# Cross-entropy over 32,000 classes: column sums of the last exps moved from ScalarE to VectorE, and the loads re-cut

## Chip, cores, metric

One core of a Trainium2 chip. The metric is the device time of one execution in microseconds (us), as a median over executions. All executions used here were with a granted clock of 1.0.

## The reference

```python
batch, num_classes = 256, 32000        # logits fp32, labels int32
log_probs = logits - np.max(logits, axis=-1, keepdims=True)
log_probs = log_probs - np.log(np.sum(np.exp(log_probs), axis=-1, keepdims=True))
return np.array([-log_probs[i, labels[i]] for i in range(batch)])
```

The logits are 32.77 MB, read once. Kernels here leave the maximum out: they compute log(sum of exp(x) times exp(-x[label])).

## The kernel before

Each of 128 partitions holds two rows in a line, 64,000 columns. They are loaded in 14 pieces ("chunks" 0 to 13), exponentiated in place by ScalarE, whose accumulator also gives the chunk's sum over its columns. The sums of the second row lie as columns in `parts[1]`; VectorE adds these up, and TensorE multiplies the sum by a diagonal matrix of exp(-x[label]), which also turns 128 partitions into one row. The last chunk's sum is added by a second, accumulating matmul. ScalarE takes the log, and 1 KB is stored.

```python
CHUNKS = [
    14848, 12288, 8832, 6528, 4992, 3776, 2752,
    2368, 1856, 1344, 1344, 1152, 1024, 896,
]
# ... tiles: chunks 0 to 4 have their own, 5 (x_mid) reuses chunk 1's, 6 to 13 (x_tail) chunk 0's

    def exps(i):
        t, base = tiles[i]
        for a, b, r in pieces[i]:
            if i == len(CHUNKS) - 1:
                acc = s_last[:, :]
            else:
                acc = parts[r][:, seen[r]:seen[r] + 1]
                seen[r] += 1
            nc.scalar.activation(
                out=t[:, a - base:b - base],
                in_=t[:, a - base:b - base],
                func=AF.Exp,
                accum_out=acc,
            )
# ... loads, labels, diag
        for i in range(2, len(CHUNKS) - 1):
            exps(i)
            # ... first row's sum, matmul and log after chunk 4
        nc.vector.reduce_sum(out=sums[:, 1:2], in_=parts[1][:, :], axis=mybir.AxisListType.X)
        nc.tensor.matmul(lane[1][:, :], sums[:, 1:2], diag[1][:, :], start=True, stop=False)
        exps(len(CHUNKS) - 1)
        nc.tensor.matmul(lane[1][:, :], s_last[:, :], diag[1][:, :], start=False, stop=True)
        log_row(1)
        # ... store
```

The softmax here doesn't subtract the row's maximum and nothing guards it: scores larger than these inputs give would overflow.

## Time and profile before

| | before |
|---|---|
| time, median | 86.03 us (85.92 to 86.08, 4 runs) |
| span of the profiled run | 84.3 us |
| ScalarE / VectorE busy | 58.9 / 0.8 us |
| last load landed (the trace's landing records) | 80.29 us |
| log of the second row starts | 82.03 us |

The span runs from the first instruction to the last on the core; the time measured outside it is some 1.7 us longer. The lines behind the table are in the prediction below. What counts is the start of the second log: what follows it (0.27 us of log, then the store and the end of the program, 2.3 us together) is the same in all kernels here. In a profile line, ACT is ScalarE, DVE VectorE, PE TensorE (PEld its loading of weights) and SP the queue that issues the loads; L95 is a line of the kernel, `out<-in` names tiles, and what stands in brackets is the idle time before the instruction and what ended it. The landing records of the trace give the moment at which each of the sixteen DMA engines reported its share of a load; a load has landed with the last of them. The "taper" below is the row of ever smaller loads at the end.

### The profile page before, as it was taken

The page shows a single profiled execution, that of the slowest core. Times are in us where ns is not written, and L with a number is a line of the kernel's source. Part 1 is how long each engine was busy: PE and PEld are TensorE (multiplying, and loading weights), DVE is VectorE, ACT ScalarE, POOL GpSimd, SP SyncE. Part 2 cuts the span into 40 slices and gives each one's busy share as a digit, 9 for nine tenths or more (in the row PEclk, how much of TensorE's full clock was granted, in tenths as well). Part 3 has the DMA queues.
Part 4 walks back from the last instruction along what each step waited for, and adds up shares of the span by engine and source line. Part 5 has one row for each costly group of instructions (what it writes and reads, how often), then busy time and mean ns, then how long its engine had stood idle before and what let it go on. Part 6 is the DMA issues. An engine that isn't in the chain of part 4 may idle for free.

```text
span 84.3 us, 126 instructions
## 1 busy us (share of the span) xinstructions
PE 1.8 (2%) x6; PEld 0.3 (0%) x6; DVE 0.8 (1%) x4; ACT 58.9 (70%) x34; POOL 3.0 (4%) x10
## 2 busy tenths in 40 slices
PE   0000000000000000000000002000000000000050
PEld 0000000000000000000000000000000000000000
DVE  0000000000000000000000200000000000000000
ACT  6000000000899999189999999999999999999960
POOL 3000000000640000000000000000000000000000
DMA  9199999998889999699998999999999999999500
GB/s 394 56 451 451 451 451 451 451 451 373 373 373 466 536 443 396 291 503 402 436 486 372 433 396 409 451 436 401 401 449 408 416 427 416 410 414 406 211 0 0
DMA packets 2226, 32.77 MB, mean 389 GB/s; under 512 B 433, under 2 KB 434, under 8 KB 1202
## 3 DMA queue, kind: packets, MB, share of 16 engines
q1 hardware_dynamic: 2018, 32.77, 91.9%
q10 hardware_dynamic: 144, 0.00, 0.1%
q0 software_dynamic: 64, 0.00, 0.1%
HBM read 32.77 MB, written 0.00 MB: 389 GB/s over the span
## 4 chain that ended last, share of the span: by engine, by line
DMA 64%; issue 13%; another core or an unknown queue 12%; SPq 4%; ACT 3%; PE 1%
DMA x<-in_logits_dram 41%; DMA x_tail<-in_logits_dram 22%; SPq L83 4%; ACT x_tail L95 3%; PE lane L143 1%; ACT res L103 0%; ACT x L95 0%; ACT eg L131 0%
## 5 line engine op out<-in xcount | busy, mean ns | idle before, releaser
L95 ACT ACTIVATE x<-x 128x14848 f32<-128x14848 f32 (+5 forms) x6 | 40.7, 6790 | 21.6 <-DMA x<-in_logits_dram 21.6
L95 ACT ACTIVATE x_tail<-x_tail 128x1344 f32<-128x1344 f32 (+6 forms) x8 | 12.2, 1525 | 0.4 <-DMA x_tail<-in_logits_dram 0.4
L95 ACT ACTIVATE x_mid<-x_mid 128x3776 f32<-128x3776 f32 x1 | 3.4, 3350 | 0.0
L118 POOL DMA_INDIRECT g<-in_logits_dram,idx x2 | 2.1, 1037 | 0.6 <-issue 0.3
L74 ACT ACT_TABLE_LOAD x1 | 1.3, 1283 | 0.7 <-PEq L162 0.7
L138 PE MATMUL lane<-diag,sums 128*1 128x128 f32 x2 | 0.6, 397 | 51.2 <-DVE sums L137 51.2
L95 ACT ACTIVATION_READ_ACCUMULATOR x_tail<-x_tail 128x1 f32 x8 | 1.5, 186 | 0.0
L141 PE MATMUL lane<-diag,sums 128*1 128x128 f32 x2 | 0.6, 394 | 28.8 <-DVE sums L140 28.8
L95 ACT ACTIVATION_READ_ACCUMULATOR x<-x 128x1 f32 x6 | 1.1, 186 | 0.0
L103 ACT ACTIVATE res<-lane 1x128 f32<-1x128 f32 x2 | 0.5, 264 | 0.7 <-PE lane L143 0.7
L133 DVE TENSOR_SCALAR diag<-ident,eg 128x128 f32<-128x128 f32 x2 | 0.5, 284 | 46.8 <-ACT eg L131 46.8
L116 POOL TENSOR_TENSOR idx<-idx,lbl 128x2 int32<-128x2 int32 x1 | 0.2, 193 | 20.1 <-DMA lbl<-in_labels_dram 20.1
L143 PE MATMUL lane<-diag,s_last 128*1 128x128 f32 x2 | 0.6, 395 | 0.2 <-ACT x_tail L95 0.2
L140 DVE TENSOR_REDUCE sums<-parts 128x1 f32<-128x11 f32 x1 | 0.2, 165 | 29.3 <-ACT x_tail L95 29.3
masks.py:199 POOL TENSOR_SCALAR_AFFINE_SELECT ident<-ident 128x128 f32<-128x128 f32 x1 | 0.3, 292 | 0.1
L138 PEld LDWEIGHTS lane<-diag,sums 128*1 128x1 f32 x2 | 0.1, 80 | 51.2 <-DVE sums L137 51.2
masks.py:197 POOL MEMSET ident<- 128x128 f32 x1 | 0.2, 194 | 0.0
L137 DVE TENSOR_REDUCE sums<-parts 128x1 f32<-128x3 f32 x1 | 0.2, 156 | 3.7 <-ACT x L95 3.7
L131 ACT ACTIVATE eg<-g 128x2 f32<-128x2 f32 x1 | 0.2, 187 | 0.0
L95 ACT ACTIVATION_READ_ACCUMULATOR x_mid<-x_mid 128x1 f32 x1 | 0.2, 186 | 0.0
L141 PEld LDWEIGHTS lane<-diag,sums 128*1 128x1 f32 x2 | 0.1, 80 | 29.3 <-DVE sums L140 29.3
L114 POOL IOTA idx<- 128x2 int32 x1 | 0.1, 121 | 0.4 <-POOLq L162 0.4
(5 smaller groups left out, 0.5 us busy)
## 6 DMA issues: line engine op xcount, KB each, us to landing
x<-in_logits_dram SPq DMA_DIRECT2D x1, 7424.0 KB, 20.6
x<-in_logits_dram SPq DMA_DIRECT2D x1, 6144.0 KB, 34.9
x<-in_logits_dram SPq DMA_DIRECT2D x1, 4416.0 KB, 44.9
x<-in_logits_dram SPq DMA_DIRECT2D x1, 3264.0 KB, 52.2
x<-in_logits_dram SPq DMA_DIRECT2D x1, 2496.0 KB, 56.9
x_mid<-in_logits_dram SPq DMA_DIRECT2D x1, 1888.0 KB, 18.1
x_tail<-in_logits_dram SPq DMA_DIRECT2D x1, 1376.0 KB
x_tail<-in_logits_dram SPq DMA_DIRECT2D x2, 672.0 KB, 27.0
```

Source lines behind the costliest of these rows:

```text
L74: nc.scalar.preload_act_table_set("natural_log_exp_and_others")
L83: nc.sync.dma_start(out=t[:, a - base:b - base], in_=flat[:, a:b])
L95: nc.scalar.activation(out=t[:, a - base:b - base], in_=t[:, a - base:b - base], func=AF.Exp, accum_out=acc,)
L103: nc.scalar.activation(out=res[0:1, r:ROWS * P:ROWS], in_=lane[r][:, :], func=AF.Ln)
L116: nc.gpsimd.tensor_add(out=idx[:, :], in0=idx[:, :], in1=lbl[:, 0:2 * ROWS:2])
L118: nc.gpsimd.indirect_dma_start(out=g[:, r:r + 1], out_offset=None, in_=logits[:, :], in_offset=bass.IndirectOffsetOnAxis(ap=idx[:, r:r + 1 ...
L131: nc.scalar.activation(out=eg[:, :], in_=g[:, :], func=AF.Exp, scale=-1.0)
L133: nc.vector.tensor_scalar_mul(diag[r][:, :], ident[:, :], eg[:, r:r + 1])
L137: nc.vector.reduce_sum(out=sums[:, 0:1], in_=parts[0][:, :], axis=mybir.AxisListType.X)
L138: nc.tensor.matmul(lane[0][:, :], sums[:, 0:1], diag[0][:, :], start=True, stop=True)
L141: nc.tensor.matmul(lane[1][:, :], sums[:, 1:2], diag[1][:, :], start=True, stop=False)
L143: nc.tensor.matmul(lane[1][:, :], s_last[:, :], diag[1][:, :], start=False, stop=True)
```

## The change

The intent: an exp with accumulator costs ScalarE an extra instruction that reads the accumulator. Six of the last exps lose it, VectorE (idle) sums their columns instead, and ScalarE, now quicker on small pieces, gets smaller last loads, so that less is left to do after the last landing. As VectorE's sum of chunk 11 and ScalarE's of 12 and 13 come late, each gets its own matmul; with that of the sum of the parts there are four.

```diff
 CHUNKS = [
-    14848, 12288, 8832, 6528, 4992, 3776, 2752,
-    2368, 1856, 1344, 1344, 1152, 1024, 896,
+    14592, 13696, 9728, 7424, 4864, 3904, 2880,
+    2112, 1408, 1152, 832, 576, 448, 384,
 ]
+ON_VECTOR = range(6, 12)
+SINGLE = 11
...
-            if i == len(CHUNKS) - 1:
-                acc = s_last[:, :]
+            if i >= SINGLE:
+                acc = single[i][:, :]
...
-            nc.scalar.activation( ... func=AF.Exp, accum_out=acc)
+            x = t[:, a - base:b - base]
+            if i in ON_VECTOR:
+                nc.scalar.activation(out=x, in_=x, func=AF.Exp)
+                nc.vector.reduce_sum(out=acc, in_=x, axis=mybir.AxisListType.X)
+            else:
+                nc.scalar.activation(out=x, in_=x, func=AF.Exp, accum_out=acc)
...
-        for i in range(2, len(CHUNKS) - 1):
+        for i in range(2, SINGLE):
...
-        exps(len(CHUNKS) - 1)
-        nc.tensor.matmul(lane[1][:, :], s_last[:, :], diag[1][:, :], start=False, stop=True)
+        for i in (11, 12, 13):
+            exps(i)
+        for i in (12, 11, 13):
+            nc.tensor.matmul(lane[1][:, :], single[i][:, :], diag[1][:, :], start=False, stop=i == 13)
```

More of the change, by code (lines that the diff above doesn't have):

```diff
@@ L58 @@
         tiles.append((tail, starts[HEAD + 1]))
-    n_of = [sum(1 for ps in pieces[:-1] for q in ps if q[2] == r) for r in range(ROWS)]
+    n_of = [sum(1 for ps in pieces[:SINGLE] for q in ps if q[2] == r) for r in range(ROWS)]
     parts = [small.tile([P, n_of[r]], F32, name=f"parts{r}") for r in range(ROWS)]
-    s_last = small.tile([P, 1], F32, name="s_last")
+    single = {i: small.tile([P, 1], F32, name=f"s{i}") for i in range(SINGLE, len(CHUNKS))}
     res = small.tile([1, ROWS * P], F32, name="res")
@@ L94, in exps @@
                 seen[r] += 1
-            nc.scalar.activation(
-                out=t[:, a - base:b - base],
-                in_=t[:, a - base:b - base],
-                func=AF.Exp,
-                accum_out=acc,
-            )
+            x = t[:, a - base:b - base]
[4 more added lines that the diff above has]
+                nc.scalar.activation(out=x, in_=x, func=AF.Exp, accum_out=acc)
     def log_row(r):
```

## The prediction

> **What bounds the kernel now.** I read the page first: its busy shares and the 40 slices, then the chain of work that ended last, then the timeline from 60 us on, which shows the end one instruction at a time. From the page:
>
> ```profile
> PE 1.8 (2%) x6; PEld 0.3 (0%) x6; DVE 0.8 (1%) x4; ACT 58.9 (70%) x34; POOL 3.0 (4%) x10
> ...
> DVE  0000000000000000000000200000000000000000
> ACT  6000000000899999189999999999999999999960
> ...
> DMA  9199999998889999699998999999999999999500
> ```
>
> The DMA row is full from the third slice to the 37th: the stream of loads sets the pace. ScalarE is full in the second half too, but only because each exp starts when its load lands. VectorE is idle, and that is what the change wants to use. The chain of waits, in order of time, says the same for the end:
>
> ```profile
> 60.24 18.96 DMA x_tail<-in_logits_dram
> 79.20 0.02 issue
> 79.22 2.14 ACT x_tail L95 x4
> 81.36 0.04 issue
> 81.41 0.60 PE lane L143 x2
> 82.01 0.02 issue
> 82.03 0.27 ACT res L103
> ```
>
> The chain is the load stream up to 79.20, the landing of the next to last load; then two exps, two accumulator reads, a matmul in two passes, the log and the store. The timeline of the end:
>
> ```profile
> 79.22 1.06 ACT L95 ACTIVATE x_tail<-x_tail 128x1024 f32<-128x1024 f32 x1
> 80.19 0.19 ACT L95 ACTIVATION_READ_ACCUMULATOR x_tail<-x_tail 128x1 f32 x1
> 80.31 0.95 ACT L95 ACTIVATE x_tail<-x_tail 128x896 f32<-128x896 f32 x1
> 80.41 0.17 DVE L140 TENSOR_REDUCE sums<-parts 128x1 f32<-128x11 f32 x1 [29.27 <-ACT x_tail L95]
> ...
> 81.17 0.19 ACT L95 ACTIVATION_READ_ACCUMULATOR x_tail<-x_tail 128x1 f32 x1
> ```
>
> The next exp starts 0.09 us after an accumulator read starts, so a read holds ScalarE for 0.093 us although it lasts 0.186. The trace's landing records put the last load at 80.29 us. So the whole end after the data is 84.3 - 80.3 = 4.0 us, of which the change touches only the last exp, its neighbours on ScalarE and the sums.
>
> **What the Trainium skill says.** (1) "ScalarE: Activation LUTs", section "What ACT_TABLE_LOAD costs": an ACTIVATE with immediate scale and bias takes 186 ns + 0.833 N, and back-to-back ones overlap by about 93 ns. The trace agrees: 4240 ns for 4864 columns is 186 + 0.8334 x 4864. (2) "VectorE: DVE Perf Modes", section "The perf-mode tier table": tensor_reduce has only a 1x program, in fp32 as in bf16; the specifications there give 0.96 GHz, so 1.04 ns a column. The two reductions of this trace, 156 ns for 3 columns and 165 ns for 11, give 9 / 8 = 1.1 ns a column and about 153 ns fixed: a short lever, but it fits 1x (8.3 ns expected) and not 2x (4.2 ns). (3) The same page, section "The TRN2 errata — SBUF-src ops pay a fixed extra latency per instruction": 58 cycles + columns for VectorE from SBUF, with a measured single duration near 150 cycles. I take the first, 60 ns, as the fixed part of the distance between two back-to-back reductions: the two multiplications for diag last 284 ns each and 0.48 us together, a distance of about 196 ns and an overlap of about 90 ns. (4) "DMA: Bandwidth & Descriptors", section "Bandwidth": transfers of 1 MiB or more for 75% of peak. The trace doesn't show such a loss in a queued stream: slices with loads of 0.45 to 1.2 MB still move 406 to 427 GB/s.
>
> **The loads.** The trace's packet records give one packet for each partition's row of a load: 59392 bytes in 2192 ns, 3584 bytes in 141 ns, so 0.0368 ns a byte and some 9 ns a packet. An engine has 8 such packets a load and one of 9 ns for the semaphore: 1.177 ns a column + 0.08 us a load. Before and after have 14 loads and 64,000 columns, so the stream ends where it did, at about 80.3 to 80.4. The issues aren't late: a load's semaphore is shared with one eight transfers earlier, and the last load may be issued once x_mid has landed, near 68.2, some 12 us before its data is due. From load 1's landing at 36.06 (27,136 columns) I get the new landings: x_mid 68.2; then the tail's eight at 71.7, 74.3, 76.0, 77.4, 78.5, 79.3, 79.9 and 80.4.
>
> **ScalarE.** An exp with accumulator takes 0.186 us + 0.833 ns a column from start to start of the next; without it 0.093 + the same. Six tail exps lose theirs: 0.56 us less work on ScalarE. Chunk 3 (7424 columns) starts at its landing, 57.78, and ends at 64.17; that is 0.6 after chunk 4 landed, as the first chunks are larger now. Then chunk 4 to 68.41, the first log to 68.63, x_mid to 72.07. The six exps without accumulator start at 72.07, 74.56, 76.41, 77.68, 78.73 and 79.52, the last two at 80.09 and 80.65. The last sum is ready for TensorE at 81.28, against 81.41 before. So the ScalarE part is worth only 0.1 us: the last exp is 0.43 us shorter (512 fewer columns), but ScalarE reaches it about 0.3 late.
>
> **VectorE.** It now has to sum 2880, 2112, 1408, 1152, 832 and 576 columns, 8960 in all, each after its exp: 9.33 us at 1.04 ns, and the fixed parts. It can't start before the first of these exps has ended, 72.07 + 2.58 = 74.65. Start of each at a distance of 1.04 ns a column + 0.06:
> - 2880 columns: 74.69, next at 77.75 (its exp had been ready at 76.51)
> - 2112: to 80.01 (exp ready 77.77)
> - 1408: to 81.54
> - 1152: to 82.81
> - 832: ends at 83.83, the fixed 0.153 counted in full because the sum of parts waits for it
> - sum of the nine parts: starts at 83.86, the next 0.07 later
> - 576 columns: 83.93 + 0.60 + 0.153 = 84.69
>
> So this engine, idle before, ends 3.3 us after the last exp. VectorE keeps up with the rate of the stream (1.04 against 1.18 ns a column), but the first piece reaches it a whole load and a whole exp late, and the taper makes the later loads come faster than it can work off that piece: 9.7 us of work have 5.6 us between 74.7 and the last landing.
>
> **TensorE and the end.** The four matmuls run in program order: sum of parts, chunk 12, chunk 11, chunk 13. The first two are done when chunk 11 comes at 84.72. One matmul's two passes take 0.59 us; two in a row add two more starts, 0.39. Chunk 13's sum has long been there. The log starts at 84.72 + 0.39 + 0.62 = 85.73, against 82.03: 3.7 us later. Log and store are as before. 85.99 + 3.7 = **89.7 us**.
>
> **Rivals.** (a) VectorE reduces fp32 at two columns a cycle. Then the reductions end at 80.8 by the same schedule, before the last exp's sum; ScalarE's 81.28 sets the end, and the time is 85.9. For it speaks only the order of the matmuls, 12 ahead of 11 but 11 ahead of 13, which would suit a VectorE that keeps pace; against it the slope of the two small reductions and the skill's table. I give it 8%. (b) Small loads slow the stream: rows of 1536 to 3328 bytes lie below all that the trace has. The packet fit leaves no room for much; even 10 ns more on each packet of the last five loads is 5 x 8 x 10 = 0.4 us, and it would be hidden behind VectorE. Alone it would make 86.3. (c) The aim of the change, ScalarE relieved and the last load short, with no new wait: at best 0.43 us, 85.6. No outcome that I can work out is faster by 2%, which would need the end 1.7 us earlier, out of 4.0 after the stream. (d) Reductions that don't overlap at all, 0.09 us more for each of four: 90.1. The other way, a fixed part smaller than I took and an ideal handover, saves some 0.4: 89.3.
>
> **Range and chances.** With 1x, the sum rests on 9.33 us of streaming, which is firm, a start at 74.7 (0.2 either way, from the landings) and small fixed parts (0.4 either way): 89.0 to 90.2 holds 8 in 10, the rivals outside counted. Slower by over 2% means over 87.7; only rival (a) or (c) avoids it. Faster 0.02, same 0.08, slower 0.90.
>
> **What would show each step.** Right: VectorE without a gap from about 74.7 to 84.7, some 10 us busy; the 2880 reduction near 3.15 us; the chain of waits ending in VectorE's reduction, the matmuls and the log instead of a load; TensorE waiting for VectorE rather than for ScalarE; the last exp ending near 81.2 with the DMA row ending in the same slice as before. Wrong: a 2880 reduction of 1.7 us (rival a), a last load that lands later than 80.6 (b), or gaps on VectorE between the reductions.

## The result

89.89 us (89.86 to 90.11, 4 runs) against 86.03: ratio 1.0456, interval 1.0436 to 1.0477, so slower. A ratio is the mean time of one kernel's fast runs over that of the other's in the same rounds, so not quite the ratio of the medians quoted.

The 40 slices of the changed kernel, of 2.2 us each, from its page:

```profile
DVE  0000000000000000000000200000000001999930
ACT  5000000004999991099999999999999999998000
...
DMA  9199999999999999698998999999899999990000
```

The DMA row is full to slice 36, which ends at 79.3 us; before, too, it ended shortly before 80 us. ScalarE (ACT) has work to slice 37. VectorE (DVE), idle before, is full in slices 35 to 38 (74.9 to 83.7 us) and busy in the next: it goes on when the loads and ScalarE are through. The end of the chain of waits, in order of time (start, duration, what):

```profile
71.96 2.50 ACT x_tail L101
74.46 0.02 issue
74.48 9.13 DVE parts L102 x5
83.62 0.02 issue
83.64 0.17 DVE sums L144
83.82 0.04 issue
83.86 0.59 PE lane L145 x2
84.45 1.29 PE lane L149 x6
85.74 0.02 issue
85.76 0.27 ACT res L107
```

Before, the load stream stood in the chain up to 79.20. Here no load stands in it after 57.6 us: from there it runs through ScalarE, and from 74.48 through VectorE's five reductions, which set the end. The groups of VectorE, each shape apart (the two numbers are busy us and mean ns):

```profile
L102 DVE TENSOR_REDUCE parts<-x_tail 128x1 f32<-128x2880 f32 x1 | 3.2, 3153 | 21.9 <-ACT x_tail L101 21.9
L102 DVE TENSOR_REDUCE parts<-x_tail 128x1 f32<-128x2112 f32 x1 | 2.3, 2343 | 0.0
L102 DVE TENSOR_REDUCE parts<-x_tail 128x1 f32<-128x1408 f32 x1 | 1.6, 1608 | 0.0
...
L102 DVE TENSOR_REDUCE s<-x_tail 128x1 f32<-128x576 f32 x1 | 0.7, 742 | 0.0
```

(3153 - 742) / (2880 - 576) = 1.05 ns a column. Only the first reduction waits for ScalarE; the zeros say that each later one found its chunk ready. Last, the timeline of the end:

```profile
80.86 0.19 ACT L104 ACTIVATION_READ_ACCUMULATOR x_tail<-x_tail 128x1 f32 x1
83.64 0.16 DVE L144 TENSOR_REDUCE sums<-parts 128x1 f32<-128x9 f32 x1
83.72 0.74 DVE L102 TENSOR_REDUCE s<-x_tail 128x1 f32<-128x576 f32 x1
...
83.86 0.59 PE L145 MATMUL lane<-diag,sums 128*1 128x128 f32 x2 [30.65 <-DVE sums L144]
...
84.24 1.49 PE L149 MATMUL lane<-diag,s 128*1 128x128 f32 x6
```

ScalarE's part is done at 80.86 + 0.19 = 81.05, earlier than before (81.17 + 0.19 = 81.36). VectorE's last sum comes at 83.72 + 0.74 = 84.46, 3.4 us after it. TensorE's eight passes (the trace has two for each fp32 matmul) then run without a gap from 83.86 on, since L149 starts with no idle time noted.

| | before | after |
|---|---|---|
| last load landed | 80.29 | 80.13 |
| ScalarE's last sum | 81.36 | 81.05 |
| VectorE's last sum | 80.57 | 84.46 |
| second log starts | 82.03 | 85.76 |

### The profile page after: what moved, and what is told of

The parts are those of the page before. It is cut to its first block, busy times and chain, and to the rows that moved or that the text cites. A ratio compares the mean times of both kernels' runs of the same rounds, so it can differ in the third digit from the quotient of the medians.

```text
span 88.1 us, 134 instructions
## 1 busy us (share of the span) xinstructions
PE 2.5 (3%) x10; PEld 0.9 (1%) x10; DVE 10.6 (12%) x10; ACT 57.7 (66%) x28; POOL 3.0 (3%) x10
## 4 chain that ended last, share of the span: by engine, by line
DMA 41%; ACT 29%; issue 13%; DVE 11%; PE 2%; SPq 0%; another core or an unknown queue 0%
DMA x<-in_logits_dram 41%; ACT x L104 22%; DVE parts L102 10%; ACT x_mid L104 4%; ACT x_tail L101 3%; PE lane L149 1%; PE lane L145 1%; ACT res L107 0%; SPq L87 0%; DVE sums L144 0%; ACT eg L135 0%
## 5 line engine op out<-in xcount | busy, mean ns | idle before, releaser
L104 ACT ACTIVATE x<-x 128x14592 f32<-128x14592 f32 (+5 forms) x6 | 43.1, 7181 | 22.9 <-DMA x<-in_logits_dram 22.8
L102 DVE TENSOR_REDUCE parts<-x_tail 128x1 f32<-128x2880 f32 (+4 forms) x5 | 9.1, 1891 | 21.9 <-ACT x_tail L101 21.9
L101 ACT ACTIVATE x_tail<-x_tail 128x2880 f32<-128x2880 f32 (+5 forms) x6 | 8.1, 1430 | 0.0
L104 ACT ACTIVATE x_mid<-x_mid 128x3904 f32<-128x3904 f32 x1 | 3.4, 3439 | 0.0
L149 PE MATMUL lane<-diag,s 128*1 128x128 f32 x6 | 1.5, 421 | 0.0
L104 ACT ACTIVATE x_tail<-x_tail 128x448 f32<-128x448 f32 (+1 forms) x2 | 1.1, 532 | 0.0
L102 DVE TENSOR_REDUCE s<-x_tail 128x1 f32<-128x576 f32 x1 | 0.7, 742 | 0.0
L149 PEld LDWEIGHTS lane<-diag,s 128*1 128x1 f32 x6 | 0.7, 120 | 0.6
L104 ACT ACTIVATION_READ_ACCUMULATOR x_tail<-x_tail 128x1 f32 x2 | 0.4, 187 | 0.0
```

The costliest lines, as they stand in the source:

```text
L101: nc.scalar.activation(out=x, in_=x, func=AF.Exp)
L102: nc.vector.reduce_sum(out=acc, in_=x, axis=mybir.AxisListType.X)
L104: nc.scalar.activation(out=x, in_=x, func=AF.Exp, accum_out=acc)
L149: nc.tensor.matmul(lane[1][:, :], single[i][:, :], diag[1][:, :], start=False, stop=i == 13)
```

## Experiments

The theory: VectorE gets 8960 columns at 1.05 ns each, the first only at 74.5, so it ends after everything else. The rivals: the smaller loads; the extra matmuls; the hand-overs between engines as such. One of the kernels is wrong; the others agree with the reference.

### All sums back on ScalarE

```diff
-ON_VECTOR = range(6, 12)
+ON_VECTOR = range(0)
```

> The changed kernel with its loads and its four matmuls, but ScalarE's accumulator sums all chunks again. Theory 'VectorE works off its backlog too late': the loss nearly goes; six accumulator reads come back on ScalarE (6 x 0.093 = 0.56 us), the eight matmul passes in one row end near 82.6 instead of 82.0, so about 86.6 us against 86.0 of the kernel before. Rival 'the small loads or the four matmuls cost it': stays above 89 us.

86.70 us (86.60 to 86.79) against 86.00, ratio 1.0078 (1.0044 to 1.0111). So 3.2 of the 3.9 us lost go with VectorE's sums, and loads and matmuls together cost 0.7. The theory's number held.

### The loads of the kernel before, sums on VectorE

```diff
-    14592, 13696, 9728, 7424, 4864, 3904, 2880,
-    2112, 1408, 1152, 832, 576, 448, 384,
+    14848, 12288, 8832, 6528, 4992, 3776, 2752,
+    2368, 1856, 1344, 1344, 1152, 1024, 896,
```

> The changed kernel with the loads of the kernel before; VectorE sums six tail chunks, now 10816 columns instead of 8960. Theory 'backlog': VectorE starts some 4 us earlier, at about 70.5, since the first of its chunks lands earlier, and ends at about 82.4 although it has 1.9 us more to do; log at 83.5, so 87.6 us: half of the loss comes from the taper, which hands VectorE its work later. Rival 'VectorE's work as such, wherever it lies': more columns, so worse than 89.9, about 91.8. Rival 'the taper as such': back to 86.0.

87.74 us (87.60 to 87.80), ratio 1.0199 (1.0167 to 1.0232). VectorE has 21% more columns and the kernel is 2.15 us faster than the changed one. Its chain of waits shows why:

```profile
68.06 2.40 ACT x_tail L101
70.45 0.02 issue
70.47 10.47 DVE parts L102 x5
80.94 0.02 issue
80.97 0.16 DVE sums L144
```

VectorE starts at 70.47 instead of 74.48: 4.0 us earlier for 1.9 us more work. What counts is when the first chunk is handed over and how many columns follow from there on. As the tail's first exp can't start before chunk 6 has landed (67.84 here, 71.54 in the changed kernel, by the landing records), a taper that leaves fewer columns for the tail also starts VectorE later.

### Half of the columns

```diff
-                nc.vector.reduce_sum(out=acc, in_=x, axis=mybir.AxisListType.X)
+                nc.vector.reduce_sum(out=acc, in_=x[:, 0:(b - a) // 2], axis=mybir.AxisListType.X)
```

> Wrong on purpose: each of the six reductions reads only the first half of its chunk's columns; same instructions, waits and matmuls as the changed kernel. Theory 'backlog of columns at one a cycle': the 2880-column reduction becomes 1.65 us, VectorE keeps pace and ends at about 80.6; the eight passes on TensorE then set the end, log at 82.2, so about 86.2 us. Rival 'handing over from ScalarE to VectorE to TensorE costs it, not the columns': stays above 88.5.

86.30 us (86.27 to 86.48), ratio 1.0028 (0.9996 to 1.0060). The sums are wrong by design: 4480 of the second row's 32,000 columns are missing, which for such random logits moves the logarithm by only about 0.15, and the comparison with the reference let that pass; agreement with it is thus a loose check here. All instructions, waits and matmuls of the changed kernel are there, and 3.6 of its 3.9 us are gone. Its timeline shows VectorE waiting for ScalarE now:

```profile
76.53 2.15 DVE L102 TENSOR_REDUCE parts<-x_tail 128x1 f32<-128x1056 f32 x2 [0.20 <-ACT x_tail L101]
78.84 1.37 DVE L102 TENSOR_REDUCE parts<-x_tail 128x1 f32<-128x576 f32 x2 [0.17 <-ACT x_tail L101]
```

So it is the columns, not the hand-overs.

### Order of the matmuls

```diff
-        nc.tensor.matmul(lane[1][:, :], sums[:, 1:2], diag[1][:, :], start=True, stop=False)
         for i in (11, 12, 13):
             exps(i)
-        for i in (12, 11, 13):
-            nc.tensor.matmul(lane[1][:, :], single[i][:, :], diag[1][:, :], start=False, stop=i == 13)
+        for i in (12, 13):
+            nc.tensor.matmul(lane[1][:, :], single[i][:, :], diag[1][:, :], start=i == 12, stop=False)
+        nc.tensor.matmul(lane[1][:, :], sums[:, 1:2], diag[1][:, :], start=False, stop=False)
+        nc.tensor.matmul(lane[1][:, :], single[11][:, :], diag[1][:, :], start=False, stop=True)
```

> The changed kernel with the two matmuls of ScalarE's sums (chunks 12 and 13) ahead of the matmul of the parts, and chunk 11's last. Theory 'the passes of TensorE stand in a row behind VectorE, 0.21 us each, and four of them needn't': log at 85.15 instead of 85.76, so about 89.3 us. Rival 'the passes lie beside VectorE's last reduction': unchanged, 89.9.

89.28 us (89.16 to 89.48), ratio 1.0383 (1.0348 to 1.0418): 0.6 us better than the changed kernel. The timeline:

```profile
80.51 1.09 PE L148 MATMUL lane<-diag,s 128*1 128x128 f32 x4 [27.36 <-ACT x_tail L104]
...
83.56 0.16 DVE L144 TENSOR_REDUCE sums<-parts 128x1 f32<-128x9 f32 x1
83.64 0.74 DVE L102 TENSOR_REDUCE s<-x_tail 128x1 f32<-128x576 f32 x1
...
84.44 0.59 PE L150 MATMUL lane<-diag,s 128*1 128x128 f32 x2
85.06 0.27 ACT L107 ACTIVATE res<-lane 1x128 f32<-1x128 f32 x1 [4.09 <-PE lane L150]
```

ScalarE's sums go through TensorE while VectorE still works, and only one matmul follows VectorE's last sum: 85.06 - 84.38 = 0.68 us from that sum to the log, against 85.76 - 84.46 = 1.30 in the changed kernel. Program order on TensorE had made two sums, ready since 81.05 or before, wait for VectorE's.

### The loads alone, and again

```diff
-ON_VECTOR = range(6, 12)
+ON_VECTOR = ()
-SINGLE = 11
+SINGLE = 13
-        for i in (11, 12, 13):
+        for i in (13,):
-        for i in (12, 11, 13):
+        for i in (13,):
```

> The loads of the changed kernel with the sums and the two matmuls of the kernel before: the taper alone. ScalarE, 0.6 us late already at chunk 4, can't catch up with the short loads when each costs it an accumulator read; the log starts about 0.2 to 0.4 us later than in the kernel before, about 86.3 us. Against the run with four matmuls and all sums on ScalarE (86.7 us) the difference of about 0.3 is the two extra matmuls. If short last loads helped by themselves: 85.6.

87.02 us, but spread from 86.49 to 87.45 over 6 runs; ratio 1.0101 (1.0064 to 1.0138). That is not the 86.3 expected. The trace's landing records show load 1's sixteen shares landing over 1.69 us (36.37 to 38.05), against 0.79 in the changed kernel; the other loads show the same lag (1.55 to 1.74). One engine's share, 0.7 us behind the fifteen others, makes most of the difference. The list of DMA issues of this run has it as time from issue to landing (last column):

```profile
x<-in_logits_dram SPq DMA_DIRECT2D x1, 6848.0 KB, 36.9
...
x<-in_logits_dram SPq DMA_DIRECT2D x1, 2432.0 KB, 61.1
```

The same kernel was therefore run again, beside the first experiment's.

> The kernel of the run with the loads alone once more, since the profile of that run shows a load stream whose slowest engine came 1.7 us after the first, against 0.8 in the others, and its times spread over 1 us. If that lag is chance of the run: now about 86.4 us with a spread below 0.4. If it belongs to this kernel: 87.0 again, with the same lag in the profile.

86.41 us (86.36 to 86.93), ratio 1.0061 (1.0041 to 1.0082), and in the list of DMA issues:

```profile
x<-in_logits_dram SPq DMA_DIRECT2D x1, 6848.0 KB, 36.0
...
x<-in_logits_dram SPq DMA_DIRECT2D x1, 2432.0 KB, 60.0
```

In this job, on another chip, the lag was gone (0.88 us for load 1), so it does not belong to the kernel as such, though the times spread over 0.57 us and not below the 0.4 expected. Why one of the sixteen DMA engines fell behind in the first job isn't known. Taken at this value, the new loads alone cost 0.4 us. ScalarE is late when the tail begins (its first exp starts at 71.76, 0.3 us after chunk 6 landed) and falls further behind: the last chunk landed at 80.02 and its exp starts at 80.89. Each small piece costs ScalarE the fixed part of an exp and an accumulator read; how much of the lateness is due to each was not tested apart.

> The run with the changed loads, four matmuls and all sums on ScalarE once more, beside the loads alone on the same chip: the two differ only in how the last sums reach TensorE. Theory: two more matmuls in a row behind the last sums cost 0.2 to 0.3 us, so 86.7 us. If matmuls beside ScalarE's last exps are free: equal to the loads alone.

86.77 us (86.61 to 87.10), ratio 1.0093 (1.0075 to 1.0110): 0.36 more in the medians than the loads alone on the same chip, 0.28 by the ratios. How long ScalarE waits for the last matmul stands in brackets, first for the loads alone, then for this run:

```profile
82.29 0.27 ACT L107 ACTIVATE res<-lane 1x128 f32<-1x128 f32 x1 [0.80 <-PE lane L149]
...
82.68 0.27 ACT L107 ACTIVATE res<-lane 1x128 f32<-1x128 f32 x1 [1.02 <-PE lane L149]
```

The two more matmuls thus cost 0.22 us at the end; of the 0.39 between the two logs, 0.16 is there before them (chunk 9's exp starts at 77.81 here, at 77.65 with the loads alone). The steps are then, in the medians: loads 0.4, matmuls 0.4 (0.2 by the profiles), VectorE 3.1, in all 3.9 us; they add up because each is the difference between neighbouring runs.

### A version meant to beat both

Loads chosen so that ScalarE is done with a chunk about when the next lands; VectorE gets only chunks 7 and 9, each reduction ending before the sums are needed; one matmul for the last chunk, as in the kernel before.

```diff
-    14592, 13696, 9728, 7424, 4864, 3904, 2880,
-    2112, 1408, 1152, 832, 576, 448, 384,
+    15296, 13248, 9536, 6976, 4672, 3968, 2816,
+    2176, 1280, 1280, 832, 768, 576, 576,
-ON_VECTOR = range(6, 12)
+ON_VECTOR = (7, 9)
-SINGLE = 11
+SINGLE = 13
-        for i in (11, 12, 13):
+        for i in (13,):
-        for i in (12, 11, 13):
+        for i in (13,):
```

> A version meant to beat both: VectorE sums only chunks 7 and 9 (3456 columns, with a load between them in which it catches up), one matmul for the last chunk as in the kernel before, and loads whose exps ScalarE can finish by the next landing (last load 576 columns). Theory 'VectorE is free of charge as long as each reduction ends before the next one is handed over': VectorE ends near 79.5, the log starts 0.2 to 0.3 us before that of the kernel before, about 85.75 us. Rival 'any sum moved to VectorE delays the sum of the parts': 86.2 or more.

85.90 us (85.74 to 86.60, 6 runs) against 85.96 (85.91 to 86.39): ratio 0.9999 (0.9967 to 1.0031), the same. In the profiled run the plan worked: VectorE's two reductions end before the sums are due and cost nothing, and the log starts at 81.71, 0.3 us earlier than before.

```profile
75.62 3.90 DVE L102 TENSOR_REDUCE parts<-x_tail 128x1 f32<-128x2176 f32 x2 [23.34 <-ACT x_tail L101]
...
80.41 0.16 DVE L144 TENSOR_REDUCE sums<-parts 128x1 f32<-128x11 f32 x1 [0.89 <-ACT x_tail L104]
...
81.71 0.27 ACT L107 ACTIVATE res<-lane 1x128 f32<-1x128 f32 x1 [0.67 <-PE lane L149]
```

> The same loads and matmuls as the version with two chunks on VectorE, but all sums on ScalarE's accumulator: what VectorE's part in that version is worth. Two more accumulator reads of 0.093 us: 0.1 to 0.2 us longer than that version, about 85.9 us. If the gain came from the loads alone, both are the same.

The same loads with all sums on ScalarE (`ON_VECTOR = ()`): 85.99 us (85.92 to 86.37), ratio 1.0000 (0.9976 to 1.0024); its log starts at 81.97. Of the 0.26 us between the two profiled logs, 0.07 is there already when x_mid's exp starts (67.62 against 67.55), and 0.19 is two accumulator reads of 0.093, as expected; in the times it is not resolved. The moved sums come to 0.1 us in the medians, less than the noise (the intervals reach 0.2 to 0.3 us either way), and no version here is shown to beat the kernel before.

## Why the prediction was right

**VectorE at 1.04 ns a column.** Predicted 3.15 us for 2880 columns and a busy stretch from 74.69 to 84.69; measured 3.153 us and 74.48 to 84.46. Halving the columns took away nearly the whole loss; that settles the columns left to VectorE as the cause. The measured 1.05 ns a column refutes rival (a), the double rate, and the overlap of 0.08 us between reductions refutes rival (d). Two small slips: "3.3 us after the last exp" should be 3.4 by the prediction's own 84.69 and 81.28 (measured: 3.4), and the 150 cycles of its point (3) are the page's fixed part of a single operation, not a whole duration; here that part is 0.14 us.

**The late start.** The prediction named the first piece's lateness, made worse by the taper, and not VectorE's rate, as the root. The run with the old loads shows this separately: more columns, an earlier start, 2.15 us less.

**The loads.** Predicted unchanged, last landing 80.3 to 80.4; measured 80.13 against 80.29. Rows of 1536 bytes brought no loss beyond the fixed time of each packet that the prediction had counted, so rival (b) is out.

**ScalarE.** Predicted 0.1 us earlier than before, measured 0.3 (81.05 against 81.36). From x_mid's exp on, everything ran 0.2 ahead of the predicted schedule (68.43 against 68.63), VectorE's start too; the lead begins with chunk 3, whose exp starts at 57.65 instead of 57.78. The lengths were right.

**TensorE, the mis-sized term.** From VectorE's last sum to the log the sum had 1.04 us (84.69 to 85.73); it is 1.30. The step "the first two are done when chunk 11 comes" failed: the passes for the sum of parts, chunk 12, chunk 11 and chunk 13 run in one row from 83.86, and chunk 11's had to wait for chunk 12's. The prediction's own figures say so: the sum of the parts ends at 83.86 + 0.16 = 84.02, and two matmuls in a row take 0.59 + 0.39, so they end at 85.0, after chunk 11's 84.72. The passes are also 0.21 us apart instead of the 0.20 taken from a single matmul: six of them take 1.29 us in the chain. This error, 0.26 us late, and VectorE's start, 0.2 us early, cancelled by luck: the log came at 85.76 where 85.73 was said, and 89.7 against 89.89 looks better than the parts are. The same error sat in the estimate for rival (a): 85.9 was said for a VectorE that keeps pace, while the run with half columns, which is that case, took 86.3, with TensorE's row as its end.

**Rival (c)**, an overall gain, did not come about even where VectorE keeps pace and ScalarE is relieved: that is the run with half of the columns, 86.3 us.

## What to carry to other kernels

An idle engine is not free capacity at the end of a pipeline: ask when it gets its first piece, and whether all that follows from there fits in the time that is left. Here 9.3 us of work were handed over 5.6 us before the last landing. Pieces moved to a slower engine should be those that it finishes before the next join, and on the engine that joins (TensorE) the operands that are ready early should stand first in program order.

## What the Trainium skill lacked or had wrong

- "VectorE: DVE Perf Modes", section "The perf-mode tier table", gives tensor_reduce as 1x without a duration. In fp32 it took 742 ns for 576 columns and 3153 ns for 2880, about 1.05 ns a column and 0.14 us fixed; five in a row took 9.12 us where their durations add up to 9.46, so each overlaps the next by 0.08 us.
- "ScalarE: Activation LUTs" mentions the accumulator output but not its price: a separate instruction of 0.19 us after each exp, holding ScalarE for 0.09 us.
- "DMA: Bandwidth & Descriptors", section "Bandwidth", advises 1 MiB or more a transfer for 75% of peak. Its table goes by the size of a transfer. Queued one behind the other, chunks 8 to 12 of the changed kernel (704 down to 224 KB, 2.26 MB in all) landed between 74.11 and 79.69 us by the trace's landing records: 405 GB/s, against 431 for chunk 3 alone (3.8 MB, from 48.81 to 57.62). So the small sizes cost some 6% in a queued stream, and not a quarter.
- "TensorE: Matmul & The Clock Gate" states 106.7 ns from start to start for 128 columns while the array is cold (bf16), and "FP8 and Floating Point Precision" four passes for a true fp32 matmul; neither puts the two together for fp32. Here one fp32 matmul of 128 columns shows as two instructions, 0.21 us apart in a row, so 0.43 us for each matmul in the row. That fits four cold passes of 106.7 ns; no run here tests that reading, and the trace gives the granted clock as 1.0 throughout, which does not speak for it.
